# A seven-product MLP that starts on activations not yet normalised, with the projection in its stream

## The chip, the cores and the metric

One core of one Trainium2 chip runs the whole program. The metric is device time in microseconds (us). TensorE (PE) does the matmuls, VectorE (DVE) and ScalarE (ACT) the elementwise work, GpSimd (POOL) a little of it, and SyncE (SP) issues most transfers.

## The reference, cut to what matters

A trunk of two layers on 1024 tokens of 1024 channels, in float32. Each layer mixes tokens, projects the mixture with `w_out` and adds it to the residual `h`, and then adds an MLP:

```
h = h + concat(main_out, mem_out) @ w_out[l]
u = rmsnorm(h, norm_mlp[l])          # per token: h * rsqrt(mean(h*h) + eps), per channel: * gain
a = relu(u @ w_up[l])                # 1024 -> 4096
h = h + (a * a) @ w_down[l]          # 4096 -> 1024
```

The factor rsqrt(...) is one positive number per token, so relu(r * z) = r * relu(z): it can be applied to the up side's outputs instead of its inputs.

## The kernel before, in words

Activations lie channel by partition. Every float32 operand of a matmul is split into a high part (ScalarE, a copy to fp32r, `split_hi`) and a low remainder (VectorE, `split_lo`), and each product takes three matmuls of 128x128 by 512 columns: hi·hi, hi·lo, lo·hi.

**Seven-product blocks.** The MLP is cut into four blocks of 1024 hidden channels (`NFB`); each is an up block and a down block. A block multiplies 1024x1024 by 1024x1024 with Strassen's seven products in the order 1, 2, 6, 5, 3, 7, 4 (`ORDER`), each a *step* of four *units* (one for each 128 output rows p); a unit is 12 matmuls (four chunks of three). A step needs four *windows* (split operand tiles), a unit needs one split weight tile. Before the split some operands are sums: weight sums (128x512, L966) and window sums (128x1024, `sums`, L836, L966; step 6 needs t3 and t2 for each of two chunk pairs, steps 5 and 4 one each). Step 6's sums need outputs of the block before from its steps 7, 3 and 2. In the first up block of a layer the windows are split and stored to DRAM; the other three up blocks fetch them (`cached`), so they do no window work.

**Outputs.** Products 1, 6, 5, 3 accumulate in four PSUM banks, 7 and 4 in four, and step 2 takes the two banks left in turn. In an up block the outputs of steps 1, 6, 5 are copied by ScalarE, those of 2, 7, 4 added by VectorE (L1016), that of 3 final in PSUM; `relu2` then applies ReLU and the square on ScalarE (L997, L1001). In a down block every output is added to `h` by VectorE (`accumulate`, L974).

**The planner.** `Stream.run` (L907) goes through the units; in each slot it emits first the output of the unit before, then pieces of work (`fill`, L891) sorted by due time, then the unit's matmuls. A piece that is due is always emitted; others up to LOOK = 16 slots early, if what they need is ready, and only while the slot's booked load stays within FULL = 2.5 on VectorE and on ScalarE. Booked costs: LO = 0.605 a split or sum of 512 columns, SUM2 = 1.137 a window sum, CPY = 0.54 a copy on ScalarE. Outputs book their load before `fill`. A weight split is due two slots ahead of its unit, and at most WP = 5 split weight tiles live; at most 16 window tiles live in the pool xp. Engines take their work in the order of emission, inside `tc.manual_schedule()`; outside of it a scheduler orders it.

**Into the MLP.** In layer 0 the projection is a seven-product block in a stream of its own (operand windows in g tiles); in layer 1 it is plain products: a first part, and a second part over three chunks, 16 units of nine matmuls (L1554 to L1563). After each output `after_mix` (L1111) splits h times gain into `xs` (ScalarE and VectorE) and adds its square to the norm (`Norm.add`: ScalarE, then POOL). The norm's sums over channels, the power and the row of factors `rowb` come with some delay from `Norm.finish`. The MLP then begins with eight *plain units* (L1026): the output rows p = 0 of the first up block, for both halves of the hidden rows and of the tokens, on `xs` with plain products, 96 matmuls; their outputs get the token factor from VectorE (L1048). Beside them VectorE makes the normalised activations `xb` (L1078, 16 products), on which the first up block goes on with p = 1, 2, 3: 21 units. The later up blocks reuse its windows and have 28.

Of the kernel before, what the change touches and what calls it, by code (L numbers as in the profile page):

```python
# [41 lines left out]
def kernel(  # L42
# [613 lines left out]
    class Piece:  # L656

        __slots__ = ("due", "emit", "dve", "act", "pre", "gap", "x", "w", "slot")
# [5 lines left out]
    x_live, turn = [0], [0]  # L664
    WP = 5
# [8 lines left out]
    class Stream:  # L674
# [4 lines left out]
        def __init__(self, windows=None, cap=16, w_live=0):  # L679
            self.steps, self.units, self.pieces, self.events = [], [], [], {}  # L680
            self.windows, self.cap, self.w_live = windows or x_live, cap, w_live
# [15 lines left out]
        def piece(self, *args, **kw):  # L697
            p = Piece(*args, **kw)
            self.pieces.append(p)
            return p  # L700
# [9 lines left out]

        def next_weights(self, wt, ws):

            n = len(self.units)
            ld = self.loads(wt, n)
            for j in range(2):
                hi, lo, box = self.split_pieces(n - 1 + j, lambda j=j: wt.at(j, 0, 0),
                                                self.stationary, [ld[j, 0]], w=1)
                lo.emit = lambda j=j, box=box, lo=lo.emit: (lo(), ws.update({(j, 0): box[0]}))
# [18 lines left out]
        def add_block(self, wt, b, fin, evac, pairs=range(4), cached=None, store=None, alloc=x_tile, b_in_x=False,  # L737
                      loaded=None):
# [8 lines left out]
            for j, m in enumerate(ORDER):  # L747
                step = SimpleNamespace(m=m, win=[None] * 4, evac=evac, pairs=pairs, lo=[])
# [14 lines left out]
                else:  # L763
                    self.sums(m, b, fin, T, wins, first)
                    n, t = {1: (0, 0), 2: (1, 0), 3: (1, 1), 4: (0, 0), 5: (None, None), 6: (0, 0), 7: (0, 1)}[m]
                    for c in range(4):
# [8 lines left out]
                        def make(step=step, c=c):  # L775
                            step.win[c] = alloc([P, 2, HALF], F32R)
                            return step.win[c]
# [98 lines left out]
        def issue(self, q, i):  # L876
            for r in q.pre:
                if isinstance(r, Piece) and r.slot is None:
                    self.issue(r, i)
            q.slot = i  # L880
            self.windows[0] += q.x
# [9 lines left out]
        def fill(self, i):  # L891
            left = []
            for q in self.pieces:
# [4 lines left out]
                elif q.due <= i + LOOK and (self.load[0] + q.dve <= FULL or not q.dve) \  # L898
                        and (self.load[1] + q.act <= FULL or not q.act) \
                        and (not q.x or self.windows[0] < self.cap) and (not q.w or self.w_live < WP) \  # L900
# [6 lines left out]
        def run(self, plain=()):  # L907

            self.pieces.sort(key=lambda q: q.due)
            held = {}  # L910
            pending = None
            n = len(self.units)
            for i in range(-len(plain), n):
                self.load, self.now = [0.0, 0.0], i
# [31 lines left out]
                def after(slot, step=step, p=p, ps=ps, kind=kind, i=i):  # L946
# [4 lines left out]
                    if i == step.last:  # L951
                        self.windows[0] -= 4
# [4 lines left out]
            while self.late or self.pieces:  # L957
# [5 lines left out]
                self.fill(10 ** 6)  # L963

# [18 lines left out]
    def mlp(l, nrm, gain, wt0, ws, hook, then=None):  # L983
        store = {m: [dr.tile([P, 2, HALF], F32, name=f"win{l}_{m}_{c}") for c in range(4)] for m in ORDER}
        st = Stream(w_live=2)
# [7 lines left out]
        def grid():  # L993
            return [[[None] * 2 for _ in range(2)] for _ in range(2)]
# [11 lines left out]
        def up_evac(blk, hid):  # L1006
            def evac(st, m, p, ps, slot):
# [5 lines left out]
                elif m == 3:  # L1013
                    relu2(st, blk, c, n, t, p, slot, ps)
                else:
                    nc.vector.tensor_tensor(c, ps, c, op=ALU.add)  # L1016
                    st.load[0] += LO
                    relu2(st, blk, c, n, t, p, slot)
            return evac


        hid0 = grid()
        plain = []
        banks = {}

        def plain_unit(hf, q):  # L1026
            work = []
            for k in (2 * q, 2 * q + 1):
                for n in range(2):
                    def mm(k=k, n=n):  # L1030
                        if k == 0:
                            kind = st.free.pop(0)
                            banks[hf, n] = (kind, bank_tile(kind))
                        x_, w, ps = xs[hf][k], ws[n, k // 4], banks[hf, n][1]
                        nc.tensor.matmul(ps, w[:, 0, k % 4, :], x_[:, 0], start=k == 0, stop=False)
                        nc.tensor.matmul(ps, w[:, 0, k % 4, :], x_[:, 1], start=False, stop=False)
                        nc.tensor.matmul(ps, w[:, 1, k % 4, :], x_[:, 0], start=False, stop=k == NK - 1)
                    work.append(mm)

            def after(slot):  # L1040
                x_live[0] -= 2
                if hf == 1 and q in (1, 3):
                    st.w_live -= 2
                if q == 3:
                    for n in range(2):
                        kind, ps = banks[hf, n]
                        r = hid_at(hid0, n, hf, 0)
                        nc.vector.scalar_tensor_tensor(r, ps, 0.0, nrm.rowb[hf], op0=ALU.max, op1=ALU.mult)  # L1048
                        st.load[0] += 0.67

                        def square(r=r, n=n):
                            nc.scalar.activation(r, r, AF.Square)
                            st.events["fin", 0, n, hf, 0] = st.now
                        st.late.append(square)
                        st.free.append(kind)
            plain.append((work, after))

        for hf in range(2):
            for q in range(4):
                plain_unit(hf, q)  # L1060
        x_live[0] = 16
        for n in range(2):
            def half_w(n=n):
                ws[n, 1] = split_w(wt0.at(n, 1, 0))
            st.piece(-8, half_w, dve=LO, act=CPY, w=1)


        xb = grid()
        made = {}
        for t in range(2):  # L1070
            for k2 in range(4):
                for i in range(2):
                    k = 2 * k2 + i

                    def norm(t=t, k2=k2, i=i, k=k):
                        if i == 0:
                            xb[k2 // 2][t][k2 % 2] = x_tile([P, 2, HALF], F32)
                        nc.vector.scalar_tensor_tensor(xb[k2 // 2][t][k2 % 2][:, i, :], h[k][:, hs(t)], gain[:, k:k + 1],  # L1078
                                                       nrm.rowb[t], op0=ALU.mult, op1=ALU.mult)
                    made[t, k2, i] = st.piece((-4 + k2 // 2) if t == 0 else (-1 + k2 // 2), norm, dve=0.67, x=1 - i,  # L1080
                                              pre=[lambda t=t: nrm.rowb[t] is not None, *([made[t, k2, 0]] if i else [])],
                                              gap=0)

        for blk in range(NFB):
            hid = grid() if blk else hid0
            wt = Weights(w_up[l], 0, blk * FB) if blk else wt0
            st.add_block(wt, lambda n, t, kk: xb[n][t][kk],
                         lambda n, t, kk: [made[t, 2 * n + kk, i] for i in range(2)],
                         up_evac(blk, hid), range(4) if blk else range(1, 4),
                         cached=store if blk else None, store=None if blk else store, b_in_x=not blk,  # L1090
                         loaded=None if blk else {nk: st.piece(-9, lambda nk=nk: wt0.load(*nk)) for nk in LOADS})
# [3 lines left out]
        with tc.manual_schedule():  # L1095
            st.run(plain)

    def split_w(src, st=Stream):
        w = st.stationary(None)
        split(src, w)  # L1100
        return w
# [6 lines left out]
    def mixed(nrm, gain):  # L1108
        return lambda st, n, hf, slot: after_mix(n, hf, nrm, gain)
# [170 lines left out]
    for n in range(NK):  # L1280
        reload(n)
    st = Stream(windows=[0], cap=8)
    st.add_block(Weights(w_out[0], 0, 0, 1), lambda n, t, kk: mixb[n][t][kk], lambda n, t, kk: [],
                 accumulate(mixed(nrm, g_mlp[0]), lambda t: 1 - t), alloc=g_tile)
    wt0, ws0 = Weights(w_up[0], 0, 0), {}
    st.next_weights(wt0, ws0)
    st.run()
# [25 lines left out]
    mlp(0, nrm, g_mlp[0], wt0, ws0, last0, mem_ahead)  # L1313
# [237 lines left out]
    wt1, ws1 = Weights(w_up[1], 0, 0), {}  # L1551
    for nk in LOADS:
        wt1.load(*nk)
    for n in range(NK):  # L1554
        raw = rawp.tile([P, 3, P], F32, tag="raw", name="raw")
        for ln, ap in out_rows(1, n):
            nc.sync.dma_start(out=raw[ln], in_=ap)
        wsel = split_unit(raw, 3)
        for hf in range(2):
            ps = mm_tile()  # L1560
            mm3(ps, wsel, lambda k, s: mix[hf][3 + k][:, s], range(3))
            nc.vector.tensor_tensor(h[n][:, hs(hf)], ps, h[n][:, hs(hf)], op=ALU.add)
            after_mix(n, hf, nrm, g_mlp[1])  # L1563
# [12 lines left out]
    ws1.update({(n, 0): split_w(wt1.at(n, 0, 0)) for n in range(2)})  # L1576
    mlp(1, nrm, g_mlp[1], wt1, ws1, last1)
# [24 lines left out]
```

## Time and profile before

| | |
|---|---|
| median of 3 runs | 1922.75 us (1922.67 to 1922.79) |
| profiled execution | 1920.99 us, span 1919.3 us |
| granted TensorE clock | 0.997 of full speed |
| matmuls | 8786 |
| HBM read, written | 196.71 MB, 46.14 MB |

The span goes from the first to the last instruction. Matmuls are pipelined: a record lasts 0.39 us while the next one starts 0.23 us later, so TensorE's loss is read from the length of a stage against its count of matmuls, and not from busy time. Queued VectorE records overlap a little in the same way.

### The profile page before, as it was taken

The numbers are of one execution on the slowest core, as the hardware profiler recorded it, in microseconds if no ns is written. First come the engines' busy times: TensorE is split into PE (matmuls) and PEld (weight loads), VectorE is DVE, ScalarE is ACT, GpSimd is POOL, SyncE is SP. The second block draws the span as 40 slices with busy tenths as digits, with TensorE's granted clock in tenths as the row PEclk, the third lists the DMA queues.
The fourth block names the chain that finished last, engine by engine and source line by source line (L and its number), as shares of the span: only waits on it lengthen the run. The fifth ranks groups of instructions, "written<-read, shape, count | busy, mean of one in ns | idle before, by whom it ended". The sixth has DMA issues, their size and how long they took to land. (4 is left out here: it accounts for less than half of the span.)

```text
span 1919.3 us, 24542 instructions
## 1 busy us (share of the span) xinstructions
PE 1875.7 (98%) x8786; PEld 1519.3 (79%) x8786; DVE 1416.0 (74%) x2577; ACT 985.9 (51%) x2063; POOL 197.4 (10%) x244
## 2 busy tenths in 40 slices
PE   8999999999999999999999999999999999999999
PEld 6867878878888888888768776787888888888887
DVE  6788899896496497489673668679885596496495
ACT  7553654843553553555453666555643643543553
POOL 4502120000000000001424221140000000000000
PEclk9999999999999999999999999999999999999999
DMA  6311423617307407411211123234546227307412
GB/s 253 110 28 52 175 78 142 263 70 278 135 23 285 154 24 262 175 55 67 88 39 39 28 73 97 62 104 197 198 161 226 96 90 262 132 24 284 153 45 66
DMA packets 139052, 244.44 MB, mean 127 GB/s; under 512 B 20852, under 2 KB 67762, under 8 KB 138930
## 3 DMA queue, kind: packets, MB, share of 16 engines
q1 hardware_dynamic: 137458, 238.15, 35.6%
q10 hardware_dynamic: 1472, 4.73, 0.6%
q8 instruction: 69, 1.13, 0.2%
q14 instruction: 53, 0.43, 0.1%
HBM read 196.71 MB, written 46.14 MB: 127 GB/s over the span
## 5 line engine op out<-in xcount | busy, mean ns | idle before, releaser
L651 ACT ACTIVATE w<-wa 128x512 fp32r<-128x512 f32 x371 | 230.9, 624 | 216.4 <-PE mm L941 99.5
L654 DVE TENSOR_TENSOR w<-wa,w 128x512 fp32r<-128x512 f32 x371 | 255.2, 688 | 100.0 <-ACT w L651 99.9
L941 PE MATMUL mm<-x,w 128*128 128x512 f32 x676 | 263.4, 390 | 1.1 <-DVE w L654 1.1
L938 PE MATMUL mm<-x,w 128*128 128x512 f32 x676 | 263.5, 390 | 0.2 <-DVE h L974 0.2
L940 PE MATMUL mm<-x,w 128*128 128x512 f32 x676 | 263.1, 389 | 0.0
L270 PE MATMUL mm<-x,w 128*128 128x512 f32 x448 | 183.4, 411 | 3.9 <-DVE h L374 2.1
L938 PE MATMUL sps<-x,w 128*128 128x512 f32 x468 | 182.8, 391 | 2.3 <-ACT x L651 2.3
L966 DVE TENSOR_TENSOR wa<-wa 128x512 f32<-128x512 f32 x264 | 181.0, 693 | 5.3 <-DMA wa<-in_w_up 4.6
L941 PE MATMUL sps<-x,w 128*128 128x512 f32 x468 | 182.5, 390 | 1.0 <-DVE w L654 1.0
L940 PE MATMUL sps<-x,w 128*128 128x512 f32 x468 | 182.1, 389 | 0.0
L272 PE MATMUL mm<-x,w 128*128 128x512 f32 x448 | 178.0, 398 | 1.0 <-DVE w L234 0.9
L271 PE MATMUL mm<-x,w 128*128 128x512 f32 x448 | 178.4, 399 | 0.4 <-DVE x L234 0.4
L941 PEld LDWEIGHTS mm<-x,w 128*128 128x128 f32 x676 | 126.9, 188 | 28.7 <-DVE w L654 2.2
L938 PEld LDWEIGHTS mm<-x,w 128*128 128x128 f32 x676 | 126.9, 188 | 26.8 <-issue 0.6
L940 PEld LDWEIGHTS mm<-x,w 128*128 128x128 f32 x676 | 126.9, 188 | 26.3
L651 ACT ACTIVATE x<-g 128x512 fp32r<-128x512 f32 x192 | 115.4, 620 | 54.9 <-DVE g L966 54.9
L654 DVE TENSOR_TENSOR x<-g,x 128x512 fp32r<-128x512 f32 x192 | 132.1, 688 | 9.1 <-ACT x L651 9.1
L974 DVE TENSOR_TENSOR h<-mm,h 128x512 f32<-128x512 f32 x124 | 85.0, 685 | 38.4 <-PE mm L941 38.4
L255 POOL TENSOR_TENSOR raw<-raw,cols 128x512 f32<-128x512 f32 x40 | 47.1, 1197 | 639.5 <-DMA raw<-in_w_in 597.5
L997 ACT ACTIVATE g<-g 128x512 f32<-128x512 f32 x90 | 56.9, 632 | 103.9 <-DVE g L1016 103.9
L270 PEld LDWEIGHTS mm<-x,w 128*128 128x128 f32 x448 | 85.0, 190 | 26.2 <-issue 5.3
L938 PEld LDWEIGHTS sps<-x,w 128*128 128x128 f32 x468 | 87.9, 188 | 21.4 <-ACT x L651 3.1
(353 smaller groups left out, 4035.5 us busy)
## 6 DMA issues: line engine op xcount, KB each, us to landing
x<-win SPq DMA_DIRECT2D x168, 512.0 KB, 6.1
wa<-in_w_up SPq DMA_DIRECT2D x32, 1024.0 KB, 5.8
wa<-in_w_down SPq DMA_DIRECT2D x32, 1024.0 KB, 5.1
win<-x SPq DMA_DIRECT2D x56, 512.0 KB, 3.0
h<-hd SPq DMA_DIRECT2D x16, 512.0 KB, 3.6
raw<-in_w_in SPq DMA_DIRECT2D x10, 512.0 KB, 3.8
g<-in_x SPq DMA_DIRECT2D x8, 512.0 KB, 6.7
raw<-in_w_mem_kv SPq DMA_DIRECT2D x8, 512.0 KB, 3.7
```

Of the source, the lines that this page charges most:

```text
L255: nc.gpsimd.tensor_tensor(r, r, gain[:, k0:k0 + n].rearrange("p (k o) -> p k o", o=1).broadcast_to([P, n, P]), op=ALU.mult)
L270: nc.tensor.matmul(ps, w0, a0, start=i == 0, stop=False)
L271: nc.tensor.matmul(ps, w0, a1, start=False, stop=False)
L272: nc.tensor.matmul(ps, w1, a0, start=False, stop=i == n - 1)
L651: nc.scalar.activation(dst[:, 0], src, AF.Copy)
L654: nc.vector.tensor_tensor(dst[:, 1], src, dst[:, 0].bitcast(F32), op=ALU.subtract)
L938: nc.tensor.matmul(ps, w[:, 0, k, :], x_[:, 0], start=m in (1, 2, 7) and k == 0, stop=False, skip_group_check=True)
L940: nc.tensor.matmul(ps, w[:, 0, k, :], x_[:, 1], start=False, stop=False, skip_group_check=True)
L941: nc.tensor.matmul(ps, w[:, 1, k, :], x_[:, 0], start=False, stop=k == 3, skip_group_check=True)
L966: eng.tensor_tensor(out_, a, b, op=op)
L974: nc.vector.tensor_tensor(c, ps, c, op=ALU.add)
L997: nc.scalar.activation(c, c if src is None else src, AF.Relu)
```

## The change

1. The eight plain units go. The first up block is a full seven-product block of 28 units, on `xb` = h times gain, not normalised: `after_mix` writes it with one ScalarE copy and no split.
2. In every up block `relu2` takes the token factor in: one VectorE operation max(z, 0) * rowb in place of ScalarE's ReLU; it books 0.67 of VectorE load. The square stays on ScalarE.
3. Layer 0: projection and MLP are one stream, so MLP pieces may be emitted in the projection's slots; the manual schedule begins at the MLP's first unit. Layer 1: the 16 units of the projection's second part become plain slots of the MLP's stream, booked with a load of 1.4 and 1.5; the first step's windows lie in g tiles.
4. Counters of live windows are kept per pool.

```diff
         def add_block(self, wt, b, fin, evac, pairs=range(4), cached=None, store=None, alloc=x_tile, b_in_x=False,
-                      loaded=None):
+                      loaded=None, pool=None, first_in_g=False):
...
+                in_g = first_in_g and j == 0
+                self.pool = ([0], 4) if in_g else pool or XPOOL
...
-        def run(self, plain=()):
+        def run(self, plain=(), ordered=0):
             self.pieces.sort(key=lambda q: q.due)
+            order = tc.manual_schedule()
...
             for i in range(-len(plain), n):
-                self.load, self.now = [0.0, 0.0], i
+                self.load, self.now = [0.0, 0.0] if i >= 0 else [1.4, 1.5], i
+                if i == ordered:
+                    order.__enter__()
...
-        def relu2(st, blk, c, n, t, p, slot, src=None):
-            nc.scalar.activation(c, c if src is None else src, AF.Relu)
-            st.load[1] += CPY
+        def relu2(st, blk, c, n, t, p, src):
+            nc.vector.scalar_tensor_tensor(c, src, 0.0, nrm.rowb[t], op0=ALU.max, op1=ALU.mult)
+            st.load[0] += 0.67
...
-        hid0 = grid()
-        plain = []
-        def plain_unit(hf, q):
...
-                    def norm(t=t, k2=k2, i=i, k=k):
...
-    def after_mix(n, hf, nrm, gain):
+    def after_mix(st, n, hf, nrm, gain, xb):
         src = h[n][:, hs(hf)]
-        xs[hf][n] = x_tile()
-        split(src, xs[hf][n], gain[:, n:n + 1])
+        kk = n % 4 // 2
+        q = xb[n // 4][hf]
+        if q[kk] is None:
+            q[kk] = x_tile([P, 2, HALF], F32)
+        else:
+            st.events["xb", n // 4, hf, kk] = st.now
+        nc.scalar.activation(q[kk][:, n % 2, :], src, AF.Copy, scale=gain[:, n:n + 1])
+        st.load[1] += CPY
         nrm.add(hf, src, n == NK - 1)
...
-    st = Stream(windows=[0], cap=8)
+    st, xb = Stream(), halves()
+    x_live[0] = 16
     st.add_block(Weights(w_out[0], 0, 0, 1), lambda n, t, kk: mixb[n][t][kk], lambda n, t, kk: [],
...
-    wt0, ws0 = Weights(w_up[0], 0, 0), {}
-    st.next_weights(wt0, ws0)
-    st.run()
+    n_out = len(st.units)
...
-    mlp(0, nrm, g_mlp[0], wt0, ws0, last0, mem_ahead)
+    mlp(0, st, nrm, xb, last0, mem_ahead)
+    st.run(ordered=n_out)
...
+    st, xb = Stream(w_live=3), halves()
+    x_live[0] = 14
...
+    def out_unit(n, hf):
+        box = []
+        def ahead():
+            if hf == 0 and n + 1 < NK:
+                wsels[n + 1] = split_unit(raws[n + 1], 3)
+                if n + 2 < NK:
+                    out_raw(n + 2)
+        def mm(k):
+            if k == 0:
+                ahead()
+                kind = st.free.pop(0)
+                box.append((kind, bank_tile(kind)))
+            w, x_, ps = wsels[n], mix[hf][3 + k], box[0][1]
+            nc.tensor.matmul(ps, w(k, 0), x_[:, 0], start=k == 0, stop=False)
...
+        def after(slot):
+            kind, ps = box[0]
+            nc.vector.tensor_tensor(h[n][:, hs(hf)], ps, h[n][:, hs(hf)], op=ALU.add)
+            st.free.append(kind)
+            after_mix(st, n, hf, nrm, g_mlp[1], xb)
...
+        plain.append(([lambda k=k: mm(k) for k in range(3)], after))
...
-    ws1.update({(n, 0): split_w(wt1.at(n, 0, 0)) for n in range(2)})
-    mlp(1, nrm, g_mlp[1], wt1, ws1, last1)
+    wt1 = Weights(w_up[1], 0, 0)
+    mlp(1, st, nrm, xb, last1, first_in_g=True,
+        loaded={nk: st.piece(-99, lambda nk=nk: wt1.load(*nk)) for nk in LOADS}, weights=wt1)
+    st.run(plain)
```

## Rows read from the trace of the kernel before

**Rows 1.** The page, busy us of each engine, share of the span, instructions.

```profile
PE 1875.7 (98%) x8786; PEld 1519.3 (79%) x8786; DVE 1416.0 (74%) x2577; ACT 985.9 (51%) x2063; POOL 197.4 (10%) x244
```

**Rows 2.** Busy time by stretch: length, then engines in the first row's order.

```profile
core 0: us, PE busy (x) PEld busy (x) DVE busy (x) ACT busy (x) POOL busy (x), PEclk, DMA share, GB/s
208.80:292.00 83.20, 79.83 (x358) 64.87 (x357) 81.68 (x118) 49.17 (x84) 18.77 (x12) 1.00 0.24 76
292.00:316.04 24.04, 24.04 (x117) 20.17 (x116) 20.04 (x32) 9.78 (x17) 2.31 (x2) 1.00 0.27 110
316.04:374.80 58.76, 58.24 (x254) 46.93 (x253) 51.57 (x80) 41.98 (x79) 0.00 (x0) 1.00 0.72 277
374.80:452.90 78.10, 76.70 (x338) 62.91 (x337) 67.91 (x105) 31.73 (x56) 0.00 (x0) 1.00 0.37 138
452.90:529.00 76.10, 76.10 (x337) 63.04 (x336) 41.72 (x64) 40.02 (x73) 0.00 (x0) 1.00 0.46 163
529.00:605.20 76.20, 76.20 (x337) 63.07 (x337) 65.79 (x103) 31.78 (x56) 0.00 (x0) 1.00 0.39 141
1251.00:1283.70 32.70, 32.70 (x145) 26.69 (x144) 27.06 (x35) 20.47 (x36) 16.63 (x12) 1.00 0.34 117
1283.70:1311.50 27.80, 26.59 (x137) 22.28 (x136) 21.75 (x35) 11.65 (x20) 2.76 (x3) 1.00 0.23 95
1311.50:1371.70 60.20, 58.62 (x254) 46.79 (x252) 53.00 (x82) 42.01 (x79) 0.00 (x0) 1.00 0.71 271
1371.70:1449.80 78.10, 76.71 (x338) 62.91 (x337) 68.79 (x106) 31.74 (x56) 0.00 (x0) 1.00 0.38 138
...
529.00:550.80 21.80, 21.80 (x97) 18.02 (x97) 21.79 (x35) 12.15 (x22) 0.00 (x0) 1.00 0.00 1
```

**Rows 3.** TensorE's waits: layer 0's projection, then layer 1's MLP start (total, times, longest).

```profile
PE sps L941 <- DVE w L654: 1.2, 1, 1.2
PE tr L277 <- POOL rstd L321: 1.2, 1, 1.2
PE sps L941 <- DVE g L654: 1.0, 1, 1.0
...
PE mm L1035 <- DVE h L1562: 1.2, 1, 1.2
```

**Rows 4.** VectorE in time: second up block's last units into the second down block.

```profile
518.36 0.69 DVE L1016 TENSOR_TENSOR g<-mm,g 128x512 f32<-128x512 f32 x1 [1.43 <-PE mm L941]
518.97 0.68 DVE L654 TENSOR_TENSOR w<-wa,w 128x512 fp32r<-128x512 f32 x1
519.57 1.22 DVE L966 TENSOR_TENSOR g<-g 128x1024 f32<-128x1024 f32 x1
521.08 0.69 DVE L1016 TENSOR_TENSOR g<-sps,g 128x512 f32<-128x512 f32 x1 [0.29 <-PE sps L941]
...
538.61 1.22 DVE L966 TENSOR_TENSOR g<-g 128x1024 f32<-128x1024 f32 x1
...
542.84 0.69 DVE L974 TENSOR_TENSOR h<-mm,h 128x512 f32<-128x512 f32 x1
```

**Rows 5.** The plain outputs with the token factor: ns min/median/max.

```profile
L1048 DVE SCALAR_TENSOR_TENSOR g<-mm,rb x6: 681/691/692, 304.7 to 1314.0; 128x512 f32<-128x512 f32 x6
```

**Rows 6.** VectorE in time: first up block's last unit into the first down block.

```profile
374.69 0.69 DVE L654 TENSOR_TENSOR x<-g,x 128x512 fp32r<-128x512 f32 x1 [1.14 <-ACT x L651]
...
377.70 1.22 DVE L966 TENSOR_TENSOR g<-g 128x1024 f32<-128x1024 f32 x1
...
385.92 1.22 DVE L966 TENSOR_TENSOR g<-g 128x1024 f32<-128x1024 f32 x1
...
390.66 0.68 DVE L974 TENSOR_TENSOR h<-mm,h 128x512 f32<-128x512 f32 x1
...
394.80 0.69 DVE L974 TENSOR_TENSOR h<-sps,h 128x512 f32<-128x512 f32 x1
```

**Rows 7.** TensorE in time: the second steps of these two down blocks.

```profile
388.15 0.39 PE L941 MATMUL mm<-x,w 128*128 128x512 f32 x1
...
391.49 0.47 PE L938 MATMUL mm<-x,g 128*128 128x512 f32 x1 [0.23 <-DVE h L974]
...
395.63 0.47 PE L938 MATMUL sps<-x,w 128*128 128x512 f32 x1 [1.17 <-ACT x L651]
...
542.41 0.39 PE L941 MATMUL mm<-x,w 128*128 128x512 f32 x1
```

More of the change, by code (lines that the diff above doesn't have):

```diff
@@ L656 @@
     class Piece:
-        __slots__ = ("due", "emit", "dve", "act", "pre", "gap", "x", "w", "slot")
+        __slots__ = ("due", "emit", "dve", "act", "pre", "gap", "x", "w", "slot", "pool")
         def __init__(self, due, emit, dve=0.0, act=0.0, pre=(), gap=1, x=0, w=0):
@@ L664 @@
     x_live, turn = [0], [0]
+    XPOOL = (x_live, 16)
     WP = 5
@@ L674, with __init__ @@
     class Stream:
-        def __init__(self, windows=None, cap=16, w_live=0):
+        def __init__(self, w_live=0):
             self.steps, self.units, self.pieces, self.events = [], [], [], {}
-            self.windows, self.cap, self.w_live = windows or x_live, cap, w_live
+            self.pool, self.w_live = XPOOL, w_live
             self.now = 0
@@ L698, in piece @@
             p = Piece(*args, **kw)
+            p.pool = self.pool
             self.pieces.append(p)
@@ L709, in loads @@
             return out_
[L711 to L718, printed above, removed]
         def split_pieces(self, due, src, make, pre, x=0, w=0):
@@ L880, in issue @@
             q.slot = i
-            self.windows[0] += q.x
+            q.pool[0][0] += q.x
             self.w_live += q.w
@@ L899, in fill @@
                         and (self.load[1] + q.act <= FULL or not q.act) \
-                        and (not q.x or self.windows[0] < self.cap) and (not q.w or self.w_live < WP) \
+                        and (not q.x or q.pool[0][0] < q.pool[1]) and (not q.w or self.w_live < WP) \
                         and self.ready(q, i):
@@ L951, in after @@
                     if i == step.last:
-                        self.windows[0] -= 4
+                        step.pool[0][0] -= 4
                 pending = after
@@ L963, in run @@
                 self.fill(10 ** 6)
+            order.__exit__(None, None, None)
     def tt(eng, out_, a, b, op):
@@ L981, in accumulate, with halves, mlp @@
         return evac
-    def mlp(l, nrm, gain, wt0, ws, hook, then=None):
+    def halves():
+        return [[[None] * 2 for _ in range(2)] for _ in range(2)]
+    def mlp(l, st, nrm, xb, hook, then=None, **first):
         store = {m: [dr.tile([P, 2, HALF], F32, name=f"win{l}_{m}_{c}") for c in range(4)] for m in ORDER}
-        st = Stream(w_live=2)
         st.then = then
@@ L1013, in evac @@
                 elif m == 3:
-                    relu2(st, blk, c, n, t, p, slot, ps)
+                    relu2(st, blk, c, n, t, p, ps)
                 else:
@@ L1017, in evac @@
                     st.load[0] += LO
-                    relu2(st, blk, c, n, t, p, slot)
+                    relu2(st, blk, c, n, t, p, c)
             return evac
-        hid0 = grid()
-        plain = []
-        banks = {}
-        def plain_unit(hf, q):
[L1027 to L1073, printed above, removed]
-                    def norm(t=t, k2=k2, i=i, k=k):
[L1076 to L1082, printed above, removed]
@@ L1084, in mlp @@
-        for blk in range(NFB):
[L1085 to L1089, printed above, removed]
+        for blk in range(NFB):
+            hid = halves()
+            st.add_block(first.pop("weights", None) or Weights(w_up[l], 0, blk * FB), lambda n, t, kk: xb[n][t][kk],
+                         lambda n, t, kk: [("xb", n, t, kk)], up_evac(blk, hid),
@@ L1090, in mlp @@
                          cached=store if blk else None, store=None if blk else store, b_in_x=not blk,
-                         loaded=None if blk else {nk: st.piece(-9, lambda nk=nk: wt0.load(*nk)) for nk in LOADS})
+                         **({} if blk else first))
             st.add_block(Weights(w_down[l], blk * FB, 0), lambda n, t, kk, hid=hid: hid[n][t][kk],
@@ L1094, in mlp @@
                          accumulate(hook if blk == NFB - 1 else None, lambda t: t))
[L1095 to L1101, printed above, removed]
     def reload(n):
@@ L1281 @@
         reload(n)
-    st = Stream(windows=[0], cap=8)
+    st, xb = Stream(), halves()
+    x_live[0] = 16
     st.add_block(Weights(w_out[0], 0, 0, 1), lambda n, t, kk: mixb[n][t][kk], lambda n, t, kk: [],
-                 accumulate(mixed(nrm, g_mlp[0]), lambda t: 1 - t), alloc=g_tile)
-    wt0, ws0 = Weights(w_up[0], 0, 0), {}
-    st.next_weights(wt0, ws0)
-    st.run()
+                 accumulate(lambda st, n, hf, slot: after_mix(st, n, hf, nrm, g_mlp[0], xb), lambda t: 1 - t),
+                 alloc=g_tile, pool=([0], 8), b_in_x=True)
+    n_out = len(st.units)
     nrm1 = Norm(rows=False)
@@ L1550, with out_raw @@
     nrm = Norm()
-    wt1, ws1 = Weights(w_up[1], 0, 0), {}
-    for nk in LOADS:
-        wt1.load(*nk)
+    st, xb = Stream(w_live=3), halves()
+    x_live[0] = 14
+    raws, wsels, plain = {}, {}, []
+    def out_raw(n):
+        raws[n] = rawp.tile([P, 3, P], F32, tag="raw", name="raw")
+        for ln, ap in out_rows(1, n):
+            nc.sync.dma_start(out=raws[n][ln], in_=ap)
+    def out_unit(n, hf):
[12 more added lines that the diff above has]
+            nc.tensor.matmul(ps, w(k, 0), x_[:, 0], start=k == 0, stop=False)
+            nc.tensor.matmul(ps, w(k, 0), x_[:, 1], start=False, stop=False)
+            nc.tensor.matmul(ps, w(k, 1), x_[:, 0], start=False, stop=k == 2)
+        def after(slot):
[3 more added lines that the diff above has]
+            after_mix(st, n, hf, nrm, g_mlp[1], xb)
+            if n == NK - 1:
+                x_live[0] -= 3
+                if hf:
+                    st.w_live -= 3
+        plain.append(([lambda k=k: mm(k) for k in range(3)], after))
     for n in range(NK):
[L1555 to L1558, printed above, removed]
         for hf in range(2):
[L1560 to L1563, printed above, removed]
+            out_unit(n, hf)
+    for n in range(2):
+        out_raw(n)
+    wsels[0] = split_unit(raws[0], 3)
     def last1(st, n, hf, slot):
```

8 lines of the change are left out of this document (2 added, 6 removed).

## The prediction

> **What bounds the kernel now.** I read the totals first: TensorE is busy 98% of the span, VectorE 74%, ScalarE 51% [rows 1]. VectorE is thus second, and what matters is where it reaches its limit. So I took the busy time per stage [rows 2]. A seven-product block has 28 units of 12 matmuls. A block that loses nothing takes 76.2 us (529.0 to 605.2), which is 76.2/336 = 0.227 us a matmul and 2.72 us a unit. From the second MLP block on, up and down blocks run at this pace. Time is lost only around the two places where a projection passes into the MLP:
> - projection of layer 0: 83.2 us, 7.0 over; VectorE is busy 81.7 of 83.2;
> - plain products: 24.0 and 27.8 us for 96 matmuls worth 21.8;
> - first up block (21 units, worth 57.2): 58.8 and 60.2 us, so 1.6 and 3.0 lost;
> - first down block: 78.1 us in both layers, 1.9 lost each.
>
> The waits say for whom [rows 3]: mostly splits and sums of VectorE, and once POOL's power for the norm. The reader is to see that TensorE sets the end and VectorE decides where it stumbles.
>
> **The change, part by part.**
>
> *Fewer matmuls.* Eight plain units per layer (96 matmuls) become seven more units (84). 24 matmuls fewer by 0.227 = 5.4 us gained. TensorE is the path there, so this counts in full.
>
> *VectorE at the entry.* Per layer it loses 16 low splits in after_mix, 16 normalising products, 4 splits of plain weights and 4 outputs of plain units (40); it gets 7 weight splits, 4 weight sums, 3 output sums and 16 outputs with the token factor (30). Queued operations of 512 columns start 0.60 us apart [rows 4], so about 6 us less per layer, beside TensorE. Of the 7.0 us lost in layer 0's projection, about 2.3 are norm matmuls and transposes, which stay; 4.7 are the three stalls of rows 3 (3.4 us) with refilling. Between none and all of them may go. Eight or more of the dropped splits stand ahead of the two VectorE stalls; the POOL wait has another cause, POOL's sums of squares, which stay. I take 3.2.
>
> *Start of the MLP.* In layer 1 TensorE waits 1.2 us for the last added projection [rows 3], because a plain product runs over all eight chunks; 1.4 with refilling. The first seven-product unit needs only four chunks of one half, and the projection's own matmuls run meanwhile. I take 1.4; bounds 0 and 1.4.
>
> *First up block.* It lost 1.6 + 3.0 us on VectorE, with 16 normalising products queued beside the sums. By the planner's costs, I add up what VectorE is given in the eight units up to the third step of the new order: four window sums (4.55), two more (2.27), eight weight sums (4.84), eight weight splits (4.84), six window splits (3.6), outputs (4.4): 24.6 us for 21.8 of matmuls. The old first down block got 26.2 there (8 weight sums, 8 weight splits, 8 window splits, 8 outputs, 6 window sums) and lost 1.9; so 24.3 pass free with the two units of lead. In layer 0 0.3 us stay, in layer 1, where weight sums can be done in the projection's slots, about 0.2. Gain 4.1; bounds 0 and 4.6. The projection's 16 units become plain slots: wsel split, DMA of raw and the 4 MB of w_up stand on SP in nearly their former order, wap slots free at the same moment, so I cost them nothing; their cover is the 32.7 us of matmuls [rows 2]; if a raw block came late, it would show as one gap of about 2 us.
>
> *ReLU moves to VectorE in all blocks, and takes a slot.* This is the part that I think decides. Each up block has 16 outputs. For each, ScalarE loses a ReLU and VectorE gets a scalar_tensor_tensor of 0.69 us, as the plain outputs had [rows 5]. That is 11 us more per up block, whose VectorE is busy only 41.7 of 76.1 [rows 2]; by busy time it is hidden. But the planner books 0.67 for it, and gives out other work only while a slot's VectorE load stays within 2.5. Look at the last four units of the second up block [rows 4]: each slot has an output sum, a weight split and one window sum for the down block (128x1024, 1.22 us): 0.605 + 0.605 + 1.137 = 2.35, within the cap, with 0.29 us idle left. With the ReLU it is 0.605 + 0.67 + 0.605 + 1.137 = 3.02, so the window sum is not issued. Three of the four sums then move behind the border, where they are due. In that stretch, the down block's first eight units, VectorE has no room: it is busy 21.8 of 21.8 us [rows 2].
>
> What this costs can be seen in the kernel before: in the *first* up block the same slots also hold a window split (0.605), the sums don't fit, and all four stand behind the border [rows 6], where the later block has one. There the first output of the second step, whose matmuls end at 388.5 (388.15 + 0.39, rows 7), is added only at 390.66 and the second at 394.80, while in the second down block the first ends at 542.8 and is added at 542.84 [rows 4, 7]. This step rotates over two free PSUM banks, so TensorE waits [rows 7]: 0.23 and 1.17 us, with refilling 1.9. Between the two cases lie three sums (3.4 us) less two weight sums that were put off (1.2) = 2.2 us of queue, just the difference of the two delays (2.1 against 0.0). In the changed kernel each of the six later down blocks stands like the first one before, and the output of the last up unit adds another 0.6 us: 1.9 + 0.6 = 2.5 each, 15.0 in all. The two first down blocks go from 1.9 to 2.5: 1.2. Bounds: nothing, if the sums find room elsewhere (the blocks of today), and 3.5 a block, if a weight sum is pushed over too and its queue time is lost twice: 6 x 3.5 + 2 x 1.6 = 24.
>
> *The rest.* ScalarE gets lighter; nobody waits for it once VectorE is the later one. The norm's chain (squares, POOL sums, power, transposes) is issued as before; its row is needed only at the second step's outputs, over 11 us after the stream reaches the MLP. DRAM copies of the windows get four more units, spread.
>
> *Sum.* Gains 5.4 + 3.2 + 1.4 + 4.1 = 14.1. Losses 15.0 + 1.2 = 16.2. Net 2.1 us longer: the profiled execution took 1920.99 us (span 1919.3 and 1.7 around it), so 1923.1; the median of the runs lies 1.76 above it, which gives 1924.8.
>
> **The rivals.**
>
> *The sums find room.* For it: an up block has 34 us of VectorE idle, and the windows of the later down blocks are made early. Against: a sum needs outputs of the sixth step, so it can't go ahead of the last four slots, and these are the full ones. Then only the 1.2 us of the first down blocks is lost: -14.1 + 1.2 = -12.9, 1909.8.
>
> *Slower, with no gain at the entry.* The plain units were 24 us in which TensorE had work and VectorE could run ahead; now the first seven-product step follows the projection at once. If VectorE's queue at the first up block's third step then decides (24.6 us of work against 24.3; it needs one operation more than I counted to lose what it lost before), the stalls move instead of going. The price: gains 5.4, losses 16.2, +10.8 and 1933.5. Against it stand the ten operations fewer. The Trainium skill ("Perfetto Trace Analysis", Optimizing Scalar/DVE Operations) says that where VectorE is saturated it may pay to hand work to ScalarE, while here ScalarE's ReLU goes to VectorE. By this rule the change runs the wrong way; the trace agrees for the border of up and down blocks alone, since in the middle of an up block VectorE is half idle.
>
> *Only the matmuls.* The down blocks hold their pace, and the stalls at the entry stay: -5.4, 1917.3. This is the change not doing what its second half is to do.
>
> **How the numbers follow.** The forecast has 0.45, with its own range 1918 to 1930 (gain 11 to 16, loss 11 to 20). The sums find room: 0.25. Slower: 0.20. Only the matmuls: 0.10. A measurement can tell about 0.2%, 3.85 us, from no change: below 1918.9 is faster, above 1926.6 slower. Faster: 0.22 of the second case, 0.06 of the fourth, 0.02 of the forecast = 0.30. Slower: 0.19 and 0.15 of the forecast = 0.34. Same: 0.36. The range for 8 in 10 goes from 1910 (the sums find room) to 1932, short of the full slower case.
>
> **What would show it.** In the profile after: 24 matmuls fewer; no window sum (128x1024) in the last four units of the second to fourth up blocks and four of them just behind; the later down blocks at 78 to 79 us instead of 76.2, with TensorE waiting in their second step; the first up blocks near 76.5 us for 28 units; no wait for the last projection output in layer 1. If the later down blocks stay at 76.2 us, the decisive step is wrong and the time is near 1910. If the first up blocks take over 79 us, the entry has become the bound.

## The result and the profile after

The changed kernel takes 1936.23 us (median, 1934.97 to 1938.26) against 1922.77: ratio 1.0067, 95% interval 1.0057 to 1.0077. It is 13.5 us slower, where 2 were forecast, and lies outside the range (1910 to 1932). The profiled execution took 1936.35 us, span 1934.5, at a granted clock of 0.996.

The page after, busy time of each engine, against [rows 1]:

```profile
PE 1877.7 (97%) x8762; PEld 1517.4 (78%) x8762; DVE 1460.2 (75%) x2653; ACT 927.8 (48%) x1955; POOL 197.7 (10%) x244
```

The 24 matmuls are gone, and 58 us of work have left ScalarE while 44 have come to VectorE. None of this tells the time; the stages do. Busy time by stretch, answering [rows 2] in its columns: layer 0's projection, first up block, first down block, second up block, second down block and its first eight units; then layer 1's projection (second part), first up block and first down block:

```profile
211.65:293.68 82.03, 79.57 (x357) 64.85 (x356) 76.64 (x111) 50.36 (x91) 17.94 (x13) 1.00 0.30 101
293.68:373.38 79.70, 79.04 (x357) 65.08 (x356) 70.65 (x108) 48.19 (x88) 2.15 (x2) 1.00 0.59 213
373.38:451.88 78.50, 76.68 (x338) 62.91 (x337) 69.08 (x107) 29.35 (x52) 0.00 (x0) 1.00 0.37 137
451.88:528.03 76.15, 76.15 (x337) 63.06 (x336) 47.95 (x75) 34.16 (x61) 0.00 (x0) 1.00 0.47 163
528.03:606.54 78.51, 76.69 (x337) 62.91 (x336) 68.97 (x107) 29.58 (x52) 0.00 (x0) 1.00 0.38 137
528.03:549.81 21.78, 19.96 (x87) 15.98 (x86) 21.65 (x33) 8.06 (x15) 0.00 (x0) 1.00 0.00 1
1258.15:1298.95 40.80, 36.43 (x146) 27.57 (x144) 22.80 (x30) 21.86 (x39) 14.66 (x11) 0.96 0.41 144
1298.95:1380.04 81.09, 81.07 (x377) 67.33 (x376) 71.59 (x111) 51.78 (x95) 3.45 (x3) 1.00 0.59 214
1380.04:1458.53 78.49, 76.70 (x337) 62.90 (x336) 67.98 (x106) 29.45 (x52) 0.00 (x0) 1.00 0.38 137
```

Read lengths first. The second down block, 76.20 before, now takes 78.51, and in its first eight units VectorE is still busy throughout while TensorE no longer is: the forecast's decisive step. The row to stop at is 1258.15: 40.80 us for a part that took 32.70 before, with TensorE and VectorE both idle in it and the clock at 0.96.

All of the difference, by stage (lengths after minus lengths before):

| stage | forecast | measured |
|---|---|---|
| layer 0: projection to first down block | -7.2 | -4.2 (161.73 against 165.95) |
| layer 1: second part of the projection | 0 | +8.1 |
| layer 1: MLP start and first up block | -6.9 | -6.9 (81.09 against 27.80 + 60.17) |
| two first down blocks | +1.2 | +0.8 |
| six later down blocks | +15.0 | +13.6 (five of 2.35, the last 1.86) |
| sum | +2.1 | +11.4 |

The spans differ by 15.2. The other 3.8 lie in the start-up (layer 0's projection begins at 211.65, not 208.83) and between the layers (342.3, not 341.2 us). Three kernels below with the changed kernel's order there (e2, e6, e7) begin at 209.57, 209.29 and 211.21 and take 343.7 to 345.6 between the layers, and the median of the runs has gone up by 13.5 only, so I take these 3.8 for variation between runs.

VectorE in time, last units of the second up block into the second down block (border at 528.03), against [rows 4]:

```profile
517.36 0.69 DVE L1017 TENSOR_TENSOR g<-mm,g 128x512 f32<-128x512 f32 x1 [0.70 <-PE mm L940]
518.08 0.69 DVE L998 SCALAR_TENSOR_TENSOR g<-g,rb 128x512 f32<-128x512 f32 x1
518.69 0.68 DVE L654 TENSOR_TENSOR w<-wa,w 128x512 fp32r<-128x512 f32 x1
520.08 0.69 DVE L1017 TENSOR_TENSOR g<-sps,g 128x512 f32<-128x512 f32 x1 [0.70 <-PE sps L940]
...
530.77 1.22 DVE L966 TENSOR_TENSOR g<-g 128x1024 f32<-128x1024 f32 x1
...
533.71 1.22 DVE L966 TENSOR_TENSOR g<-g 128x1024 f32<-128x1024 f32 x1
...
536.65 1.22 DVE L966 TENSOR_TENSOR g<-g 128x1024 f32<-128x1024 f32 x1
...
539.59 1.22 DVE L966 TENSOR_TENSOR g<-g 128x1024 f32<-128x1024 f32 x1
...
544.33 0.68 DVE L974 TENSOR_TENSOR h<-mm,h 128x512 f32<-128x512 f32 x1
```

Ahead of the border each unit holds an output sum, the new ReLU (L998) and a weight split, and then VectorE is idle for 0.70 us; all four window sums stand behind it. The first output of the second step, whose matmuls end at 541.80, is added at 544.33. TensorE in that step, against [rows 7]:

```profile
541.41 0.39 PE L940 MATMUL mm<-x,w 128*128 128x512 f32 x1
...
545.16 0.47 PE L937 MATMUL mm<-x,w 128*128 128x512 f32 x1 [0.64 <-DVE h L974]
...
549.30 0.47 PE L937 MATMUL mm<-x,g 128*128 128x512 f32 x1 [1.17 <-ACT x L651]
```

Those are the two waits that the first down block had before, the first of them 0.4 us longer. The waits of the whole kernel after (total, times, longest), against [rows 3]:

```profile
PE sps L937 <- DVE h L974: 3.2, 4, 1.3
...
PE sps L1508 <- ACT w L233: 2.5, 1, 2.5
```

The wait for the last added projection output in layer 1 (1.2 us) is gone. New are waits for VectorE's additions (two of 1.29 and 1.17 us in layer 0's projection), and one for ScalarE's split of a projection weight in layer 1's. Around this one, ScalarE, TensorE and SP in time:

```profile
1268.40 0.52 ACT L233 ACTIVATE w<-raw 128x384 fp32r<-128x384 f32 x1 [4.00 <-DMA raw<-in_w_out]
```

```profile
1266.08 0.39 PE L1510 MATMUL sps<-x,w 128*128 128x512 f32 x1
1268.98 0.50 PE L1508 MATMUL sps<-x,w 128*128 128x512 f32 x1 [2.51 <-ACT w L233]
...
1271.33 0.63 PE L1508 MATMUL sps<-x,w 128*128 128x512 f32 x1
1271.76 0.63 PE L1509 MATMUL sps<-x,w 128*128 128x512 f32 x1
...
1273.55 0.39 PE L1508 MATMUL pv<-x,w 128*128 128x512 f32 x1
```

```profile
1242.31 1.25 SPq L1491 DMA_DIRECT2D raw<-in_w_out  x2
1253.58 2.39 SPq L640 DMA_DIRECT2D wa<-in_w_up  x4
1256.08 30.06 SPq L1491 DMA_DIRECT2D raw<-in_w_out  x12
```

The same part of SP's queue in the kernel before:

```profile
1234.92 10.29 SPq L1557 DMA_DIRECT2D raw<-in_w_out  x6
1246.19 2.52 SPq L640 DMA_DIRECT2D wa<-in_w_up  x4
1250.06 18.25 SPq L1557 DMA_DIRECT2D raw<-in_w_out  x8
```

A block of the projection's weights (two transfers) feeds two units, 4.1 us. Before, three blocks (six transfers) were issued in this stretch ahead of the 4 MB of up weights, now one. The next block comes behind 4 MB, TensorE waits 2.5 us for its split, and after the gap the 12 matmuls from 1268.98 take 4.57 us instead of 2.72, eight of them 0.43 us apart.

This comes from one line of the change that I had read without weighing it. Before, `with tc.manual_schedule()` stood around the MLP's stream alone, and the projections lay outside. Now `run()` calls `tc.manual_schedule()` at its head and enters it at the MLP's first unit. The instruction order shows the program's own order from the call on, not from the entry: projections included. So item 3 of the change, by which the manual schedule begins at the MLP's first unit, does not hold. Outside, instructions had been moved on their engines' queues. In layer 1 that had brought two blocks of weights ahead of the 4 MB; in layer 0, whose first matmul stood at 208.83, two window sums ahead of it and two more around it:

```profile
201.99 2.48 DVE L966 TENSOR_TENSOR x<-x 128x1024 f32<-128x1024 f32 x2
...
208.36 2.48 DVE L966 TENSOR_TENSOR x<-x 128x1024 f32<-128x1024 f32 x2 [2.12 <-ACT x L1262]
```

### The profile page after: what moved, and what is told of

The parts are those of the page before. It is cut to its first block, busy times and chain, and to the rows that moved or that the text cites. A ratio compares the mean times of both kernels' runs of the same rounds, so it can differ in the third digit from the quotient of the medians.

```text
span 1934.5 us, 24464 instructions
## 1 busy us (share of the span) xinstructions
PE 1877.7 (97%) x8762; PEld 1517.4 (78%) x8762; DVE 1460.2 (75%) x2653; ACT 927.8 (48%) x1955; POOL 197.7 (10%) x244
## 3 DMA queue, kind: packets, MB, share of 16 engines
q1 hardware_dynamic: 137458, 238.15, 35.5%
## 4 chain that ended last, share of the span: by engine, by line
PE 77%; DVE 13%; issue 2%; ACT 2%; DMA 2%; POOL 1%; SPq 1%; DVEq 0%; ACTq 0%; POOLq 0%
PE mm L937 10%; PE mm L940 9%; PE mm L939 9%; PE sps L940 6%; PE sps L937 6%; PE sps L939 6%; PE mm L270 4%; PE mm L272 4%; PE mm L271 4%; PE pv L937 3%; PE pv L940 3%; PE pv L939 3%; PE tr L277 2%; DVE wa L966 2%; DVE x L654 2%
## 5 line engine op out<-in xcount | busy, mean ns | idle before, releaser
L651 ACT ACTIVATE w<-wa 128x512 fp32r<-128x512 f32 x381 | 236.0, 623 | 201.3 <-PE mm L940 82.5
L654 DVE TENSOR_TENSOR w<-wa,w 128x512 fp32r<-128x512 f32 x381 | 264.9, 695 | 62.8 <-ACT w L651 62.7
L937 PE MATMUL mm<-x,w 128*128 128x512 f32 x712 | 278.1, 391 | 3.5 <-DVE h L974 3.2
L939 PE MATMUL mm<-x,w 128*128 128x512 f32 x712 | 277.1, 389 | 0.0
L940 PE MATMUL mm<-x,w 128*128 128x512 f32 x712 | 277.1, 389 | 0.0
L937 PE MATMUL sps<-x,w 128*128 128x512 f32 x476 | 186.0, 391 | 4.1 <-ACT x L651 3.5
L940 PE MATMUL sps<-x,w 128*128 128x512 f32 x476 | 185.4, 389 | 0.4 <-DVE w L654 0.4
L939 PE MATMUL sps<-x,w 128*128 128x512 f32 x476 | 185.3, 389 | 0.0
L270 PE MATMUL mm<-x,w 128*128 128x512 f32 x400 | 164.4, 412 | 4.9 <-ACT h L372 2.4
L1002 ACT ACTIVATE g<-g 128x512 f32<-128x512 f32 x128 | 80.9, 632 | 166.0 <-DVE g L998 166.0
L271 PE MATMUL mm<-x,w 128*128 128x512 f32 x400 | 159.8, 400 | 0.7 <-DVE x L234 0.4
L272 PE MATMUL mm<-x,w 128*128 128x512 f32 x400 | 159.4, 400 | 0.9 <-DVE w L234 0.9
L937 PEld LDWEIGHTS mm<-x,w 128*128 128x128 f32 x712 | 133.7, 188 | 33.4 <-issue 5.9
L940 PEld LDWEIGHTS mm<-x,w 128*128 128x128 f32 x712 | 133.7, 188 | 27.9
L939 PEld LDWEIGHTS mm<-x,w 128*128 128x128 f32 x712 | 133.6, 188 | 27.3
L937 PEld LDWEIGHTS sps<-x,w 128*128 128x128 f32 x476 | 89.3, 188 | 24.1 <-ACT x L651 4.7
L940 PEld LDWEIGHTS sps<-x,w 128*128 128x128 f32 x476 | 89.3, 188 | 19.4 <-DVE w L654 0.8
```

Source lines behind the costliest of these rows:

```text
L270: nc.tensor.matmul(ps, w0, a0, start=i == 0, stop=False)
L271: nc.tensor.matmul(ps, w0, a1, start=False, stop=False)
L272: nc.tensor.matmul(ps, w1, a0, start=False, stop=i == n - 1)
L651: nc.scalar.activation(dst[:, 0], src, AF.Copy)
L654: nc.vector.tensor_tensor(dst[:, 1], src, dst[:, 0].bitcast(F32), op=ALU.subtract)
L937: nc.tensor.matmul(ps, w[:, 0, k, :], x_[:, 0], start=m in (1, 2, 7) and k == 0, stop=False, skip_group_check=True)
```

## The experiments

Seven kernels, each against the kernel before, measured beside it (1922.4 to 1923.0 us):

| kernel | median us | ratio, 95% interval | later down blocks | layer 0 projection | layer 1 second part |
|---|---|---|---|---|---|
| changed | 1936.23 | 1.0067 [1.0057, 1.0077] | 78.5 | 82.0 | 40.8 |
| e1_relu_only | 1940.78 | 1.0096 [1.0079, 1.0113] | 78.5 | as before | as before |
| e2_unbooked | 1922.06 | 0.9993 [0.9984, 1.0003] | 76.2 | 82.1 | 40.3 |
| e3_late_order | 1924.64 | 1.0009 [1.0000, 1.0018] | 78.5 | 78.8 | 32.8 |
| e4_both | 1911.44 | 0.9937 [0.9923, 0.9952] | 76.2 | 78.8 | 32.9 |
| e5_unbooked_all | 1910.81 | 0.9943 [0.9927, 0.9960] | 76.2 | 78.7 | 32.9 |
| e6_held_loads | 1935.75 | 1.0067 [1.0052, 1.0082] | 78.5 | 82.0 | 40.1 |
| e7_loads_behind_three | 1932.61 | 1.0052 [1.0035, 1.0069] | 78.5 | 82.0 | 36.4 |

**The ReLU alone, in the kernel before** (e1_relu_only; multiplied by ones in place of the token factor):

```diff
-            nc.scalar.activation(c, c if src is None else src, AF.Relu)
-            st.load[1] += CPY
+            nc.vector.scalar_tensor_tensor(c, c if src is None else src, 0.0, ones.broadcast_to([P, HALF]), op0=ALU.max, op1=ALU.mult)
+            st.load[0] += 0.67
```

> The kernel before with one part of the change alone: in the up blocks ReLU is done by VectorE (max with 0, times a column of ones), booked 0.67, in place of ScalarE. Theory A (the planner's cap pushes three window sums behind the border of up and down blocks): the six later down blocks go from 76.2 to about 78.5 us, the two first ones from 78.1 to 78.5, 14.6 us in all, 1937 us. Theory B (the down blocks lose for another reason, the new stream's order or pools): down blocks as before, 1923 to 1925 us.

1940.78, as theory A had it, and more. All eight down blocks take 78.5 us (the last 84.46, before 82.60), and the first up blocks, which already lost time [rows 2], grow from 58.7 and 60.2 to 60.1 and 61.6. By stages 14.4 + 2.8 = 17.2 us; 17.8 by the medians. Moving the ReLU is thus slower by itself, with nothing else changed.

**The ReLU unbooked from the second block on** (e2_unbooked). Only the planner's account changes, no operation:

```diff
-            st.load[0] += 0.67
+            st.load[0] += 0.67 if blk == 0 else 0.0
```

> The changed kernel, but in the second to fourth up blocks ReLU's VectorE operation books no load. Theory A (the booking alone pushes the sums away): one window sum a slot again in the last four units of an up block, later down blocks back at 76.2 us, six times 2.3 = 13.9 us less than the changed kernel, 1922 us. Theory C (VectorE has no room there: 0.6 + 0.6 + 0.6 + 1.14 = 2.94 us of work for a unit of 2.72): the queue is only pushed a little, the down blocks still lose 1 to 2 us each, 1928 to 1934 us.

14.2 us faster than the changed kernel. Busy time of e2's second down block, and of its first eight units:

```profile
526.00:602.16 76.16, 76.16 (x337) 63.06 (x336) 66.44 (x105) 30.49 (x53) 0.00 (x0) 1.00 0.38 142
526.00:547.78 21.78, 21.78 (x98) 18.03 (x97) 21.75 (x35) 10.13 (x18) 0.00 (x0) 1.00 0.01 2
```

Three window sums are back ahead of the border at 526.00; VectorE of e2 in time:

```profile
517.26 1.22 DVE L966 TENSOR_TENSOR g<-g 128x1024 f32<-128x1024 f32 x1
...
520.32 1.22 DVE L966 TENSOR_TENSOR g<-g 128x1024 f32<-128x1024 f32 x1
...
523.39 1.22 DVE L966 TENSOR_TENSOR g<-g 128x1024 f32<-128x1024 f32 x1
```

So it was not the 0.69 us of work that cost 13.6 us, but the 0.67 booked against a cap of 2.5. With the sum such a unit holds 0.61 + 0.67 + 0.61 + 1.14 = 3.02 us for 2.72 of matmuls, and the units of lead carry the rest. Theory C fell; the projection stages kept their lengths (82.1 and 40.3 us), so what they lose has another cause.

**The manual schedule created at the MLP's first unit** (e3_late_order):

```diff
-            order = tc.manual_schedule()
+            order = None
...
                 if i == ordered:
+                    order = tc.manual_schedule()
                     order.__enter__()
```

> The changed kernel, but the region in which the engines keep the order of emission is created where the MLP's units begin and not at the head of run, so that the scheduler may order the projection's slots again. Theory D (the projection of layer 1 loses its time because its weight transfers and splits now keep the order of emission, behind 4 MB of MLP weights): the projection's second part goes from 44 us (with its gaps) back to about 33 to 36, no wait of 2.5 us for ScalarE's split, window sums of layer 0's projection ahead of its first unit; 7 to 9 us less, 1928 us. Theory E (the new slots are too full for ScalarE and VectorE in any order): 1934 to 1937 us.

11.6 us faster than the changed kernel: theory D, and beyond it. (The part that the expectation puts at 44 us is the one of 40.80 above.) The second part of layer 1's projection in e3:

```profile
1254.16:1286.99 32.83, 32.83 (x145) 26.96 (x144) 25.25 (x31) 22.48 (x40) 14.90 (x11) 1.00 0.51 183
```

TensorE is busy throughout. The gain is 8.0 there and 3.2 in layer 0's projection, whose VectorE in the changed kernel, and then in e3, begins like this:

```profile
213.23 0.69 DVE L654 TENSOR_TENSOR g<-x,g 128x512 fp32r<-128x512 f32 x1 [7.33 <-ACT g L651]
...
215.04 1.22 DVE L966 TENSOR_TENSOR x<-x 128x1024 f32<-128x1024 f32 x1
...
217.98 1.22 DVE L966 TENSOR_TENSOR x<-x 128x1024 f32<-128x1024 f32 x1
```

```profile
202.07 2.48 DVE L967 TENSOR_TENSOR x<-x 128x1024 f32<-128x1024 f32 x2
...
208.44 2.48 DVE L967 TENSOR_TENSOR x<-x 128x1024 f32<-128x1024 f32 x2 [2.12 <-ACT x L1195]
```

In the changed kernel VectorE stands idle for 7.33 us and then does the four window sums one in each slot, where the outputs have to be added; in e3, as before the change, two are done ahead and two around the first matmul (208.91).

**Both** (e4_both: the two edits above together).

> Both edits of the two kernels before this one together. If both theories hold, the gains add: 1936.2 - 13.9 - 8 = 1914 us, 0.4% faster than the kernel before the change. If either falls, 1922 or more.

1911.44, faster than either kernel. Of the two gains' sum, 14.2 + 11.6 = 25.8, 24.8 come together: the two add up to within 1 us. Its page, to set beside the first one:

```profile
PE 1866.6 (98%) x8762; PEld 1515.3 (79%) x8762; DVE 1459.8 (77%) x2653; ACT 929.1 (49%) x1955; POOL 196.8 (10%) x244
```

VectorE's busy time is that of the changed kernel within 0.4 us. 25 us lie in where the operations stand.

**Unbooked in the first blocks too** (e5_unbooked_all: e4 without the booking line).

> The late order and no booking of the ReLU in the planner in any block (so far the first block of each layer kept it). The two first down blocks still take 78.5 us. Theory A (the booking also keeps sums behind the border there, as the prediction had it for the later blocks): the first down blocks fall to between 76.2 and 77 us, 2 x 1.5 to 2.3 us less, and the time is 1907 to 1908.5 beside 1911.4 with the first block booked. Theory F (VectorE has no room at this border: the last slots of the first up block then hold a window split, an output sum, a ReLU, a weight split and a window sum, 0.6 + 0.6 + 0.67 + 0.6 + 1.14 = 3.6 us of work for a unit of 2.72): the delay only moves ahead of the border, the first up block grows by what the down block gives back, and the time is 1911 to 1914.

1910.81, no difference that could be told from e4. The first down blocks of both layers:

```profile
369.61:447.93 78.32, 76.70 (x338) 62.92 (x336) 68.97 (x107) 29.36 (x52) 0.00 (x0) 1.00 0.37 138
1361.16:1439.48 78.32, 76.70 (x338) 62.91 (x336) 68.16 (x106) 29.47 (x52) 0.00 (x0) 1.00 0.37 137
```

Neither theory had it quite. The booking is not what holds the sums there, so A falls; but nothing moved ahead of the border either, so the up block didn't grow (79.69; 79.70 in the changed kernel) as F expected. Without the booking such a slot still holds 3 x 0.605 + 1.137 = 2.95 > 2.5, as in the kernel before [rows 6], and only one weight sum came forward (0.17 us). Whether a higher cap would help at this border was not tried.

**The 4 MB held back** (e6_held_loads, e7_loads_behind_three: the changed kernel, order kept, loads of layer 1's up weights not before eight, or twelve, slots ahead of the MLP):

```diff
-        loaded={nk: st.piece(-99, lambda nk=nk: wt1.load(*nk)) for nk in LOADS}, weights=wt1)
+        loaded={nk: st.piece(-99, lambda nk=nk: wt1.load(*nk), pre=[lambda: st.now >= -8]) for nk in LOADS}, weights=wt1)
```

> The changed kernel with its order of emission kept, but the four loads of 1 MB of the up weights of layer 1 held back until eight slots before the MLP, so that ten of the fourteen output-projection loads stand ahead of them in SP's queue. Nothing else is changed; the down blocks stay at 78.5 us and the projection block of layer 0 at 82.0. If the late transfers are the whole cause of the 8 us lost in the second part of layer 1's projection (40.8 us, 32.7 before): 32.8 us and a time of 1928. If it is the transfer for the first gap and the low clock behind it only (2.7 + 12 x 0.2 + refilling, about 5 us): 36 to 38 us and 1931 to 1933. If the place of the weight splits in ScalarE's and VectorE's queues is the whole cause: 40 us and 1936, with the gaps still at the splits though the data is there.

40.1 us and 1935.75: the number of the third case, but not its reason. SP and TensorE of e6:

```profile
1270.97 2.76 SPq L640 DMA_DIRECT2D wa<-in_w_up  x4
1274.58 6.16 SPq L1491 DMA_DIRECT2D raw<-in_w_out  x4
```

```profile
1287.54 0.50 PE L1508 MATMUL mm<-x,w 128*128 128x512 f32 x1 [4.10 <-ACT w L233]
```

The gap has gone along with the 4 MB: whichever block is issued behind them is late; TensorE waits 4.10 us here. I had taken the 4 MB out of the way of blocks 2 to 5 and put it in the way of blocks 6 and 7, which are issued only when their turn comes. So this run does not separate the causes by its time. e7 puts the 4 MB where the scheduler had them, behind block 3:

> The changed kernel with its order of emission kept; only the four loads of 1 MB of up weights in layer 1 are held back a little, so that the output-projection weights of blocks 1 to 3 stand ahead of them in SP's queue and those of blocks 4 to 7 behind (in the changed kernel block 1 stands ahead, and 2 to 7 behind; held back to behind block 5, the gap of 4.1 us and the clock at half level came with block 6 in place of block 2). Each block feeds two units, 4.1 us of matmuls. Theory P (place in SP's queue): the block behind the 4 MB lands some 12 to 15 us after their issue at about 1252, so at 1264 to 1267, and is needed only at about 1273; no gap at a transfer and no 12 matmuls at 0.43 us; the second part is 33.5 to 35.5 us in place of 40.8, with gaps of 0.4 to 0.7 us at VectorE's splits left, and the time is 1929 to 1932. Theory O (the order on ScalarE and VectorE, whatever the transfers do): over 39 us and 1935 to 1937. The down blocks stay at 78.5 us and layer 0's projection block at 82.0.

The second part in e7, and what is left of its waits:

```profile
1259.05:1295.41 36.36, 34.41 (x146) 26.57 (x144) 22.50 (x30) 21.81 (x39) 14.34 (x11) 1.00 0.42 151
```

```profile
PE sps L1510 <- DVE w L234: 0.8, 1, 0.8
...
PE mm L1508 <- ACT w L233: 0.6, 1, 0.6
```

Theory P in kind: no wait for a transfer, clock 1.00, 4.4 us less (3.6 by the medians). In size it fell short of 33.5 to 35.5. The remaining 3.5 us against e3 are gaps at weight splits. SP has the same order of weight loads in both and TensorE the same matmuls; what differs is the place of splits and sums on VectorE and ScalarE. Of the 8 us, 4.4 are thus the place of the transfers (the gap of 2.67 and the 1.85 lost in the 12 matmuls behind it make 4.5) and 3.5 the place of operations on these two engines; which single one of them counts was not tried. The trace of e7 points at VectorE's splits of the projection's weights (128x384, L234). One takes 0.56 us while POOL is idle, but five of the six in this part take 0.84 to 1.68, each while POOL adds squares (L305); four of the six gaps end 0.05 us after such a split, and they make 2.4 of the 3.5 us. In e3 three splits are as slow (1.33 to 1.65), but TensorE waits for none of them: they stand further ahead of their matmuls.

## Why the prediction was wrong

- **Later down blocks** (+15.0): right, with its mechanism. 2.35 each in place of 2.5, the last one 1.86, which e1 shows alone and e2 takes away by the booking alone.
- **First down blocks** (+1.2): 0.8. Right in kind.
- **Matmuls, MLP start and first up block in layer 1** (-6.9): -6.9. The wait for the last projection output went, and no stall is left in the up block: TensorE is busy 81.07 of its 81.09 us. So the slower rival's condition ("If VectorE's queue at the first up block's third step then decides") did not come. The sign "first up blocks near 76.5 us" was set wrong: the norm's 20 and 40 small matmuls and transposes, which stood among the plain units before (x117 and x137 for 96 in [rows 2]), now stand in these blocks (x357 and x377 for 336), which take 79.70 and 81.09 us. Over 79 us thus does not mean, as the prediction has it, that the entry has become the bound. (Its sum of 24.6 us of VectorE work there is 24.5 by its own terms; nothing hangs on it.)
- **The step that failed: "The projection's 16 units become plain slots: wsel split, DMA of raw and the 4 MB of w_up stand on SP in nearly their former order, ... so I cost them nothing."** The order was not the former one, because the call at the head of `run()` keeps the program's order in the projection as well. The price was +8.1. Its "if a raw block came late, it would show as one gap of about 2 us" named the right sign (2.67 us), but not the slow matmuls behind it (1.85) nor the gaps at the splits (3.5). I had read the code for which instructions are issued, and the queue of before for their order, without asking who had made that order.
- **Layer 0, projection to first down block** (-7.2): -4.2, for the same reason. With the order left free e3 takes 158.5 us there (208.91 to 367.43), which is -7.4; the estimate was right for the kernel that I thought I had.

e3 is the change as the prediction took it to be, and it takes 1924.64; the forecast was 1924.8. That the two agree so closely is luck: by stages e3 comes to -0.2 (-7.4, +0.1, -7.3, +0.8, +13.6) where +2.1 was forecast, and its median is up by 1.7; the rest lies outside these stages (its profile has 344.2 us between the layers, 341.2 before). But no term of it was off by over 2 us. The slower rival (1933.5) came near the time for a reason it did not give.

## What to carry to other kernels

Before costing a moved step at nothing, ask whose order it had: if a scheduler had hoisted its loads and sums, putting the step under a fixed order costs what the hoisting gave, here 11.6 us without one operation more. And where a planner gives out work by booked loads, an added operation costs what its booking displaces at the next tight border, not its duration: the same operations cost 14 us or nothing with one number changed.

## What the runs showed of the hardware

A gap of TensorE can be followed by a stretch at half clock. After the gap of 2.67 us in the changed kernel and of 4.26 us in e6, the next 12 matmuls took 4.57 us in place of 2.72, and the granted clock of these 8 us was 0.79, that is, a few matmuls at 1.2 GHz between stretches at 2.4; after a gap of 2.21 us in e2 it stayed at 1.00, and 12 matmuls took 3.00:

```profile
1268.00:1276.00 8.00, 7.02 (x23) 5.51 (x24) 5.92 (x9) 4.02 (x8) 2.83 (x2) 0.79 0.09 25
```

```profile
1262.00:1270.00 8.00, 6.41 (x26) 4.82 (x27) 6.13 (x9) 4.24 (x8) 2.83 (x2) 1.00 0.09 25
```

(Changed kernel, then e2.) The length of the gap alone does not decide it. Between the two MLPs all of these kernels have a gap of 2.27 to 2.39 us ahead of the same transposes; with 2.27 us each, the granted clock behind it was 1.00 in the kernel before (976 to 981) and the changed one (983 to 988), and 0.66 in e5 (972 to 977) and e7 (983 to 988). Nor is the half clock all loss for its stage: e2, with the same order, took 40.29 us for the part that took 40.80, since at full clock TensorE came sooner to splits that were not ready (waits of 0.83, 0.82 and 0.49 us at the three splits that follow, where the changed kernel has none, 0.39 and 0.55).

A small transfer issued behind large ones on SP's queue here waited for them: the last of the four loads of 1024 KB, issued at 1255.11, landed 12.7 us later, and the next block, whose first 96 KB were issued right behind at 1256.08, could be split at 1268.40 only.
